# A float32 transformer encoder layer: where the last weight matrix is prepared, and how far ahead its raw pieces are loaded

## The chip, the cores and the metric

The kernel runs on one core of one Trainium2 chip. The metric is the time of one execution on the device in microseconds (us). The kernel before took 1673.07 us in the median of three runs (1670.78 to 1673.4).

## The reference, cut to what matters

One encoder layer runs on two sequences of 512 tokens, with a model width of 1024, all in float32. Three branches are computed from a common projection (a state space scan, a differential attention, and a cross attention to 256 memory tokens), gated, projected up and summed, and a gated feed-forward network with 2816 hidden units follows.

```python
def _layer(x, mem, l, p):
    xn = _rmsnorm(x, p['norm_mix'][l])
    mn = _rmsnorm(mem, p['norm_mem'][l])
    h = xn @ p['w_in'][l]
    u, q, k, v, xq, g = jnp.split(h, IN_SPLITS, axis=-1)
    y_s5 = _s5_branch(u, ...)                       # scan, gelu, GLU
    ...                                             # rope on q, k; differential attention
    mk, mv = jnp.split(mn @ p['w_mem_kv'][l], 2, axis=-1)
    y_x = _cross_attention(xq, mk, mv)
    merged = None
    for n in range(N_BRANCH):
        term = jax.nn.sigmoid(g[..., n * D_MODEL:(n + 1) * D_MODEL]) * (branches[n] @ p['w_up'][l, n])
        merged = term if merged is None else merged + term
    x = x + merged @ p['w_out'][l]
    xn2 = _rmsnorm(x, p['norm_ffn'][l])
    gate, up = jnp.split(xn2 @ p['w_ffn_in'][l], 2, axis=-1)
    return x + (jax.nn.silu(gate) * up) @ p['w_ffn_out'][l]
```

## The kernel before, in words

**Precision.** Matmuls take float32 operands as two parts, a rounded one and the rest (`wh`/`wl`, `xh`/`xl`), and a product is three matmuls: high by high, low by high, high by low. The helper `split` (L120 to L133) makes the two parts: the rounded one on ACT (L128, or L131 where a scale goes in), the rest on DVE (L129 or L132). All matmuls pass through one line, L61.

**Stages, in program order.** The scan branch; the gates (`gates`, products for the sigmoid gates that go to DRAM as `gD`); the GLU of the scan branch (four tiles, L460 to L469, `sg` to `bD`); the cross attention (35 steps, L618 to L655); the projections `q` and `k` of the differential attention, which are rotated (`rotated`, L672 to L686); the differential attention; the merge of the three branches; the output projection; the first feed-forward product (22 tiles `i`, L1050 to L1088); the second feed-forward product, which uses `w_ffn_out`.

**The prepared matrix.** The second feed-forward product multiplies 2 by 2 blocks with seven products instead of eight. For it `w_ffn_out` is needed as 36 pieces `(m, p)`, each of seven blocks: three of the four quadrants and four sums and differences of them, split in two parts each. The generator `prepare` (L399) makes one piece after another and stores it to DRAM (`wD`), from where the second product reads it hundreds of us later. One piece is:
- two loads into `raw` (L405, L406, 128 KB each, on SP's queue);
- a split of three quadrants into `hl` (128x3x128, thus 128x384 elements): ACT L131, then DVE L132; a store of 384 KB;
- four adds and subtracts on POOL, in place in `raw` (L415 to L418);
- a split of all four blocks of `raw` into a second `hl` (128x4x128, 128x512 elements): ACT L131, DVE L132; a store of 512 KB.

`raw` has one buffer, and so have the two `hl`. The generator stops (`yield`) once after the loads and once after the adds, so a piece is two half-pieces; each `half_piece()` call sets the next one into the program. The table `NPREP` says how many pieces are done by the end of the cross attention and how many by the end of the merge.

**Where half-pieces stand before.** Seven beside the seven last gate units, four beside the GLU tiles, 29 beside the 35 steps of the cross attention: 20 pieces. Eight in the merge of branch 2 (the loop `while queue`, L849 to L851), eight in the merge of branch 1 (L863 to L866): 8 pieces. Sixteen in the tiles 1 to 16 of the first feed-forward product: 8 pieces. Whatever is then left in the generator must be none.

**What sets the order.** Each engine runs its instructions in an order that a scheduler fixes when the program is built, from the written order, the pools and its costs. A tile that has no free buffer waits for the last reader of the buffer. After the cross attention PE goes on with the first rotated projection, into an accumulator bank (`bkmm`) that an earlier projection filled; that bank is free when its reader on DVE, the `stream_shuffle` of `rotated` (L681), has run:

```python
            V.tensor_tensor(out=t1, in0=o, in1=rope[0], op=ALU.mult)      # L679
            V.stream_shuffle(t2, o, mask)                                 # L681
            PO.tensor_tensor(out=t2, in0=t2, in1=rope[1], op=ALU.mult)    # L682
            PO.tensor_tensor(out=t1, in0=t1, in1=t2, op=ALU.add)          # L683
            split(hl[0][:, cs], hl[1][:, cs], t1, scale=0.125 if is_q else None)
```

**The merge.** A merge unit (`merge_units`, L707) is one of eight column tiles of one branch: 12 matmuls into each of two banks; DVE multiplies the gate `gl` by the two banks (L716, which frees the banks); POOL adds the result to `mg` (L720, 128x1024). The units of branch 2 have two banks for the products, those of branch 1 have six.

**The end of the first feed-forward product.** `quad_sums` (L899 to L902) makes the sums `ts` from the activations of the tiles 0 to 3 for the second product. Its pool `ts` opens where the pool `pq` of the preparation closes.

Of the kernel before, what the change touches and what calls it, by code (L numbers as in the profile page):

```python
# [10 lines left out]
F32 = mybir.dt.float32  # L11
# [8 lines left out]
P = 128  # L20
# [15 lines left out]
          (2, 6, 9), (3, 7, 9))  # L36
NPAIR = 9

NPREP = (20, 28)

NG = (7, 5, 7)
ROUND = 12582912.0
# [25 lines left out]
def encoder(ctx: ExitStack, tc: tile.TileContext, a, out):  # L68
# [88 lines left out]
    def proj(src, hi, lo, nk=KD, seqs=(0, 1)):  # L157


        wh, wl = weight(src, nk * P)  # L160
        outs = []
        for s in seqs:
            cs = slice(s * L, (s + 1) * L)
            outs.append(bank())
            for k in range(nk):
                mm3(outs[-1:], wh, wl, [(hi[k][:, cs], lo[k][:, cs])], k, nk)
        return outs
# [21 lines left out]
    def factor(ss, n, nt=4, bias=epsc):  # L189

        rs = rp.tile([P, 4], F32, tag="rs", name="rs", bufs=4)
        S.activation(out=rs[:, :nt], in_=ss[:, :nt], func=AF.Sqrt, scale=1.0 / n, bias=bias)
        V.reciprocal(rs[:, :nt], rs[:, :nt])
        bc = aux()
        for t in range(nt):
            PE.transpose(bc[:, t * P : (t + 1) * P], rs[:, t : t + 1].broadcast_to([P, P]), ident)
        return rs, bc
# [106 lines left out]
    _, bc = factor(ss0, DM)  # L304
# [12 lines left out]
    with yielding(last_s):  # L317
        x_norm(0, bc, range(6, 8))
        _, bc = factor(ss1, DM)
# [47 lines left out]
    def gates(n):  # L367

        for _ in range(n):
            t = next(todo)  # L370
            o = proj(a["w_in"][20 + t], xh, xl)
            gt = slot("ld", name="gt")
            for s in range(NS):
                cs = slice(s * L, (s + 1) * L)
                S.activation(out=gt[:, cs], in_=o[s], func=AF.Tanh, scale=0.5)
            nc.sync.dma_start(gD[t], gt)
# [19 lines left out]
    pieces = [(m, p) for m, lo_, hi_ in VISITS for p in range(lo_, hi_)]  # L396
    wD = {mp: drp.tile([P, 7, 2, P], F32, name=f"wD{mp[0]}_{mp[1]}") for mp in pieces}

    def prepare(es_, pieces_):  # L399
        pq = es_.enter_context(tc.tile_pool(name="pq", bufs=1, side="right", reuse_waits="tile"))  # L400
        for m, p in pieces_:
            raw = pq.tile([P, 4, P], F32, tag="raw", name="raw")
            f = slice(2 * p * P, (2 * p + 2) * P)
            with queued():
                nc.sync.dma_start(raw[:, 1:3], a["w_fo"][m, :, f].rearrange("p (a n) -> p a n", n=P))  # L405
                nc.sync.dma_start(raw[:, 0::3], a["w_fo"][m + 4, :, f].rearrange("p (a n) -> p a n", n=P))  # L406
            yield
            for j, w_ in ((4, raw[:, 1:4]), (0, raw)):
                n = w_.shape[1]
                hl = pq.tile([P, n, 2, P], F32R, tag=f"hl{n}", name="hl")  # L410
                split(hl[:, :, 0], hl[:, :, 1], w_, scale=0.5)
                nc.sync.dma_start(wD[m, p][:, j : j + n], hl.bitcast(F32))
                if j:
                    a21, a11, a12, a22 = (raw[:, i] for i in range(4))
                    PO.tensor_tensor(out=a22, in0=a21, in1=a22, op=ALU.add)  # L415
                    PO.tensor_tensor(out=a21, in0=a11, in1=a21, op=ALU.subtract)
                    PO.tensor_tensor(out=a11, in0=a22, in1=a11, op=ALU.subtract)
                    PO.tensor_tensor(out=a12, in0=a12, in1=a11, op=ALU.subtract)  # L418
                    yield

    def half_piece(behind_=()):
        with ExitStack() as es_:
            for i_ in behind_:
                es_.enter_context(tc.issue_after(i_.ins))
            return next(prep, None)
# [6 lines left out]
    for t in range(4):  # L432
# [9 lines left out]
        for s in range(NS):  # L442
            split(*(z_[t][:, s * L : (s + 1) * L].rearrange("p (j c) -> p j c", j=T) for z_ in (zh, zl)), yt[:, :, s, :], scale=0.5)
        zs.append(yt)
    pes = ExitStack()
    prep = prepare(pes, pieces[: NPREP[0]])
    next(prep)
    for _ in range(NG[2]):
        gates(1)
        half_piece()  # L450
    with behind():

        mrs = cst.tile([P, 4], F32, name="mrs")
# [6 lines left out]
    for t in range(4):  # L460
        o = proj(a["w_glu"][t], zh, zl, 4)
        sg = slot("zt", name="sg")
        for s in range(NS):
            S.activation(out=sg[:, s * L : (s + 1) * L], in_=o[s], func=AF.Tanh, scale=0.5, bias=bh[:, t : t + 1])
        for s in range(NS):
            g_ = sg[:, s * L : (s + 1) * L].rearrange("p (j c) -> p j c", j=T)
            V.scalar_tensor_tensor(out=g_, in0=g_, scalar=1.0, in1=zs[t][:, :, s, :], op0=ALU.add, op1=ALU.mult)
        nc.sync.dma_start(bD[0, t], sg)
        half_piece()  # L469
    phase.close()  # L470

    last_x = None
# [57 lines left out]
    xa = phase.enter_context(tc.tile_pool(name="xa", bufs=2, reuse_waits="tile"))  # L530
    xcol = phase.enter_context(tc.tile_pool(name="xcol", bufs=2, reuse_waits="tile"))

# [82 lines left out]
    for i in range(-AHEAD, len(steps) + 1):  # L618
# [24 lines left out]
        if i > 0 and steps[i - 1][2] == 3:  # L643
            h, s, _ = steps[i - 1]
# [201 lines left out]
    aes.close()  # L846
    prep = prepare(pes, pieces[NPREP[0] : NPREP[1]])
    next(prep)
# [14 lines left out]
    for m in range(KD):  # L863
        for _ in merge_units(1, b1, m, last=True):
            pass
        half_piece()  # L866
    assert next(prep, None) is None
    pes.close()

# [180 lines left out]
    for i in range(KFF):  # L1050
# [6 lines left out]
        if i == 1:  # L1057
            prep = prepare(pes, pieces[NPREP[1] :])
            next(prep)
# [11 lines left out]
        if i == 0:  # L1071
            for s in range(NS):
                _, bc = rstd(accs[s], DM)
# [539 lines left out]
```

## Time and profile before

| | |
|---|---|
| median of three runs | 1673.07 us |
| the profiled execution's own time | 1672.37 us |
| its span (first to last instruction) | 1670.6 us |
| mean granted TensorE clock | 0.984 |
| PE busy | 1595.8 us (96%) |
| DVE busy | 1180.5 us (71%) |
| ACT busy | 634.0 us (38%) |
| POOL busy | 554.0 us (33%) |
| DMA | 259.60 MB, mean 155 GB/s |

The span is cut into instructions of five engines: PE (matmuls, line L61), DVE, ACT, POOL and SP, which issues the DMAs. "Busy" counts only the time in which an engine executes. A row of a timeline has the start in us from the span's start, the duration in us, the engine, the line, the operation and the tiles (output <- inputs), the shapes, and in square brackets how long the engine sat idle before it and what ended that. A row of the waits has the engine and its instruction, what it waited for, the total in us, the number of times and the longest. A row of the windows has the window, its length, the busy time of PE, PEld (weight loads), DVE, ACT and POOL (instructions in brackets), the granted clock, the busy share of the DMA engines and GB/s.

### The profile page before, as it was taken

The numbers are of one execution on the slowest core, as the hardware profiler recorded it, in microseconds if no ns is written. First come the engines' busy times: TensorE is split into PE (matmuls) and PEld (weight loads), VectorE is DVE, ScalarE is ACT, GpSimd is POOL, SyncE is SP. The second block draws the span as 40 slices with busy tenths as digits, with TensorE's granted clock in tenths as the row PEclk, the third lists the DMA queues.
The fourth block names the chain that finished last, engine by engine and source line by source line (L and its number), as shares of the span: only waits on it lengthen the run. The fifth ranks groups of instructions, "written<-read, shape, count | busy, mean of one in ns | idle before, by whom it ended". The sixth has DMA issues, their size and how long they took to land.

```text
span 1670.6 us, 21694 instructions
## 1 busy us (share of the span) xinstructions
PE 1595.8 (96%) x7812; PEld 1315.4 (79%) x7812; DVE 1180.5 (71%) x1860; ACT 634.0 (38%) x1130; POOL 554.0 (33%) x444
## 2 busy tenths in 40 slices
PE   7999999998996699999999998999999999999997
PEld 5788788787895578877877886888888888788887
DVE  7956996255664377676568656988988888886455
ACT  6534313245453245565323434323332322321222
POOL 0001100031122322020066343665666665354242
PEclk9999999999998799999999999999999999999999
DMA  9354344768555211125577542343333322797632
GB/s 363 119 165 154 121 135 128 236 207 277 169 170 186 80 35 54 42 70 174 172 251 234 163 139 71 111 147 130 107 114 110 120 89 86 271 328 246 223 117 101
DMA packets 109354, 259.60 MB, mean 155 GB/s; under 512 B 14016, under 2 KB 42432, under 8 KB 109248
## 3 DMA queue, kind: packets, MB, share of 16 engines
q1 hardware_dynamic: 109248, 258.23, 46.0%
q8 instruction: 61, 1.00, 0.3%
q14 instruction: 45, 0.37, 0.1%
HBM read 174.85 MB, written 83.33 MB: 155 GB/s over the span
## 4 chain that ended last, share of the span: by engine, by line
PE 74%; DVE 10%; DMA 7%; ACT 3%; issue 2%; POOL 2%; SPq 1%; DVEq 0%; POOLq 0%; ACTq 0%
PE bkmm L61 63%; PE bktr L61 3%; DMA raw<-in_w_fo 3%; PE bksc L61 2%; PE bkoo L61 2%; PE bktr L64 2%; DVE wl L129 1%; DVE hl L132 1%; DMA yt<-bD 1%; PE bktr L1466 1%; ACT hl L131 1%; DVE st L1484 1%; ACT wh L128 1%; PE bktr L1437 1%; DVE tl L129 1%
## 5 line engine op out<-in xcount | busy, mean ns | idle before, releaser
L61 PE MATMUL bkmm<-xh,wh 128*128 128x512 f32 x640 | 256.8, 401 | 30.5 <-DVE t L681 27.2
L61 PE MATMUL bkmm<-xh,wl 128*128 128x512 f32 x640 | 251.8, 394 | 2.3 <-DVE wl L129 2.3
L61 PE MATMUL bkmm<-xl,wh 128*128 128x512 f32 x640 | 251.7, 393 | 0.0
L61 PE MATMUL bkmm<-tl,wh 128*128 128x512 f32 (+1 forms) x621 | 242.1, 390 | 3.5 <-DVE tl L129 3.5
L61 PE MATMUL bkmm<-th,wh 128*128 128x512 f32 (+1 forms) x621 | 242.2, 390 | 0.0
L61 PE MATMUL bkmm<-th,wl 128*128 128x512 f32 (+1 forms) x621 | 240.4, 389 | 0.6 <-DVE wl L129 0.6
L128 ACT CAST wh<-wf 128x1024 fp32r<-128x1024 f32 (+1 forms) x133 | 117.6, 884 | 196.6 <-PE bkmm L61 127.8
L129 DVE TENSOR_TENSOR wl<-wf,wh 128x1024 fp32r<-128x1024 f32 (+1 forms) x133 | 149.2, 1122 | 42.9 <-ACT wh L128 34.6
L61 PEld LDWEIGHTS bkmm<-xh,wh 128*128 128x128 f32 x640 | 120.9, 189 | 62.7 <-DVE t L681 27.9
L415 POOL TENSOR_TENSOR raw<-raw 128x128 f32<-128x128 f32 x36 | 24.2, 671 | 409.3 <-DVE hl L132 363.5
L61 PEld LDWEIGHTS bkmm<-xh,wl 128*128 128x128 f32 x640 | 120.9, 189 | 29.9 <-DVE wl L129 3.2
L61 PEld LDWEIGHTS bkmm<-tl,wh 128*128 128x128 f32 x621 | 117.1, 189 | 28.4 <-DVE tl L129 4.6
L61 PE MATMUL bkmm<-th,w 128*128 128x512 f32 x432 | 139.2, 390 | 0.1
L61 PEld LDWEIGHTS bkmm<-xl,wh 128*128 128x128 f32 x640 | 121.1, 189 | 22.5 <-issue 0.4
L61 PEld LDWEIGHTS bkmm<-th,wh 128*128 128x128 f32 x621 | 117.1, 189 | 25.0 <-ACT wh L128 1.2
L61 PEld LDWEIGHTS bkmm<-th,wl 128*128 128x128 f32 x621 | 116.7, 188 | 25.0 <-DVE wl L129 1.0
L132 DVE SCALAR_TENSOR_TENSOR hl<-raw,hl 128x384 fp32r<-128x384 f32 x72 | 76.6, 1064 | 77.3 <-ACT hl L131 76.8
L1081 POOL TENSOR_TENSOR up<-up,acc 128x512 f32<-128x512 f32 x44 | 84.6, 1942 | 93.7 <-DVE up L1027 93.7
L61 PEld LDWEIGHTS bkmm<-th,w 128*128 128x128 f32 x432 | 81.1, 188 | 17.7 <-DVE up L1027 0.8
L484 ACT ACTIVATE e<-bksc,nb 128x512 f32<-128x512 f32 (+1 forms) x96 | 58.6, 613 | 70.0 <-DVE nb L479 50.3
L61 PE MATMUL bkmm<-tl,w 128*128 128x512 f32 x216 | 84.1, 389 | 0.0
L131 ACT ACTIVATE hl<-raw 128x384 fp32r<-128x384 f32 x72 | 41.3, 573 | 103.6 <-DMA raw<-in_w_fo 68.4
(628 smaller groups left out, 3562.3 us busy)
## 6 DMA issues: line engine op xcount, KB each, us to landing
wf<-in_w_in SPq DMA_DIRECT2D x40, 512.0 KB, 3.9
wD<-hl SPq DMA_DIRECT2D x36, 512.0 KB, 2.9
w<-wD SPq DMA_DIRECT2D x36, 512.0 KB, 4.8
wD<-hl SPq DMA_DIRECT2D x36, 384.0 KB, 2.3
w<-wD SPq DMA_DIRECT2D x36, 384.0 KB, 3.4
gD<-gt SPq DMA_DIRECT2D x24, 512.0 KB, 2.9
gl<-gD SPq DMA_DIRECT2D x24, 512.0 KB, 4.3
wf<-in_w_fg SPq DMA_DIRECT2D x22, 512.0 KB, 3.5
```

Of the source, the lines that this page charges most:

```text
L61: return self.put(self.eng.matmul(*args, **kw))
L64: return self.put(self.eng.transpose(*args, **kw))
L128: h = S.copy(hi, src)
L129: l_ = V.tensor_tensor(out=lo, in0=src, in1=hi.bitcast(F32), op=ALU.subtract)
L131: h = S.activation(out=hi, in_=src, func=AF.Copy, scale=scale)
L132: l_ = V.scalar_tensor_tensor(out=lo, in0=src, scalar=scale, in1=hi.bitcast(F32), op0=ALU.mult, op1=ALU.subtract)
L415: PO.tensor_tensor(out=a22, in0=a21, in1=a22, op=ALU.add)
L484: last_x = S.activation(out=e, in_=sc, func=AF.Exp, bias=nb, scale=scale, accum_out=sm)
L1081: PO.tensor_tensor(out=up, in0=up, in1=accs[s], op=ALU.mult)
L1437: PE.matmul(kp[64 * hf : 64 * hf + 48, g * 144 : (g + 1) * 144], l_[:, 2 * hf + g, :], o_[:, 4 * g4 + 2 * hf + g, :], start=(l_ is lr48), ...
L1466: PE.matmul(ps[:, g * P : (g + 1) * P], w_[:, gg * P : (gg + 1) * P], u_[:, 8 * o + gg, :], start=True, stop=True)
L1484: V.tensor_tensor(out=sv[:, :, :, i], in0=p_, in1=q_, op=ALU.add)
```

## The change

`NPREP` goes from (20, 28) to (16, 27). The generator is opened just before the cross attention, and the gates and the GLU have no half-pieces beside them. `raw` gets two buffers, the first piece's loads are issued when the generator is opened, and the loads of piece n+1 are issued before the splits of piece n. The generator now also stops after the second half of a piece. So 32 half-pieces stand in the cross attention (16 pieces); the merge has 8 in its loop of branch 2 and up to 14 beside the units of branch 1 (11 pieces); the feed-forward tiles 1 to 18 have one each (9 pieces). What is loaded, computed and stored is the same in all.

```diff
-NPREP = (20, 28)
+NPREP = (16, 27)
...
     def prepare(es_, pieces_):
         pq = es_.enter_context(tc.tile_pool(name="pq", bufs=1, side="right", reuse_waits="tile"))
-        for m, p in pieces_:
-            raw = pq.tile([P, 4, P], F32, tag="raw", name="raw")
+        raws = []
+
+        def load(m, p):
+            raw = pq.tile([P, 4, P], F32, tag="raw", name="raw", bufs=2)
             f = slice(2 * p * P, (2 * p + 2) * P)
             with queued():
                 nc.sync.dma_start(raw[:, 1:3], a["w_fo"][m, :, f].rearrange("p (a n) -> p a n", n=P))
                 nc.sync.dma_start(raw[:, 0::3], a["w_fo"][m + 4, :, f].rearrange("p (a n) -> p a n", n=P))
-            yield
+            raws.append(raw)
+
+        load(*pieces_[0])
+        yield
+        for n_, (m, p) in enumerate(pieces_):
+            raw = raws[n_]
+            if n_ + 1 < len(pieces_):
+                load(*pieces_[n_ + 1])
             for j, w_ in ((4, raw[:, 1:4]), (0, raw)):
                 n = w_.shape[1]
...
                     PO.tensor_tensor(out=a12, in0=a12, in1=a11, op=ALU.subtract)
-                    yield
+                yield
...
-    pes = ExitStack()
-    prep = prepare(pes, pieces[: NPREP[0]])
-    next(prep)
-    for _ in range(NG[2]):
-        gates(1)
-        half_piece()
+    gates(NG[2])
...
         nc.sync.dma_start(bD[0, t], sg)
-        half_piece()
     phase.close()
...
+    pes = ExitStack()
+    prep = prepare(pes, pieces[: NPREP[0]])
+    next(prep)
...
         for _ in merge_units(1, b1, m, last=True):
             pass
         half_piece()
+        if m < 6:
+            half_piece()
     assert next(prep, None) is None
     pes.close()
```

The scheduler's orders of the two programs are nearly the same on PE. On the other engines they differ above all at three places. (Numbers behind a tile's name count the tiles of one program and are no line numbers; lines after L530 stand some lines further down in the changed program.)

**ACT at the end of the cross attention**, before: `hl` are splits of pieces, `xpTh` the transposed probabilities of the cross attention, `xosb` its last output copy, `rh` the first rotated projection.

```order
L131 ACTIVATE hl_4733<-raw_4685 128x3x128
L128 CAST wh_5339<-wf_5337 128x1024
L128 CAST xpTh_5138<-bktr_5209 128x2x128
L131 ACTIVATE hl_4795<-raw_4685 128x4x128
L653 COPY xosb_5221<-bkoo_5214 128x512
L131 ACTIVATE hl_4834<-raw_4799 128x3x128
L131 ACTIVATE hl_4887<-raw_4799 128x4x128
L131 ACTIVATE hl_4938<-raw_4891 128x3x128
L131 ACTIVATE hl_4989<-raw_4891 128x4x128
L131 ACTIVATE hl_5038<-raw_4993 128x3x128
L131 ACTIVATE hl_5091<-raw_4993 128x4x128
L131 ACTIVATE rh_5244<-t1_5246 128x512
```

ACT in the changed program, at the same place:

```order
L131 ACTIVATE hl_5089<-raw_5008 128x3x128
L659 COPY xosb_5086<-bkoo_5079 128x512
L487 ACTIVATE e_5104,sm_5105<-bksc_5097,nb_5101 128x256
L128 CAST xpTh_5066<-bktr_5117 128x2x128
L131 ACTIVATE hl_5128<-raw_5008 128x4x128
L128 CAST xpTh_5066<-bktr_5138 128x2x128
L128 CAST wh_5279<-wf_5277 128x1024
L128 CAST xpTh_5066<-bktr_5149 128x2x128
L659 COPY xosb_5161<-bkoo_5154 128x512
L131 ACTIVATE rh_5184<-t1_5186 128x512
```

Before, six splits (three pieces) stand between the last copy of the cross attention and the first rotated part, and DVE has the six second halves of them in the same place. In the changed program none stands there, on ACT or on DVE, and DVE has the first pair L679/L681 of `rotated` ahead of its last `xpTl` (the rest of the transposed probabilities).

**DVE in the merge units of branch 2**, before: `gl` frees a bank, `hl` is a piece's split, `wl` the rest of a weight tile.

```order
L716 SCALAR_TENSOR_TENSOR gl_7936<-gl_7936,bkmm_7944 128x512
L132 SCALAR_TENSOR_TENSOR hl_8017<-raw_7933,hl_8017 128x4x128
L716 SCALAR_TENSOR_TENSOR gl_7936<-gl_7936,bkmm_7958 128x512
L129 TENSOR_TENSOR wl_8030<-wf_8027,wh_8029 128x512
L716 SCALAR_TENSOR_TENSOR gl_7981<-gl_7981,bkmm_7989 128x512
L132 SCALAR_TENSOR_TENSOR hl_8061<-raw_8021,hl_8061 128x3x128
L716 SCALAR_TENSOR_TENSOR gl_7981<-gl_7981,bkmm_8003 128x512
L129 TENSOR_TENSOR wl_8075<-wf_8072,wh_8074 128x512
```

and in the changed program:

```order
L722 SCALAR_TENSOR_TENSOR gl_7876<-gl_7876,bkmm_7884 128x512
L132 SCALAR_TENSOR_TENSOR hl_7960<-raw_7873,hl_7960 128x4x128
L132 SCALAR_TENSOR_TENSOR hl_8004<-raw_7912,hl_8004 128x3x128
L722 SCALAR_TENSOR_TENSOR gl_7876<-gl_7876,bkmm_7898 128x512
L129 TENSOR_TENSOR wl_7970<-wf_7967,wh_7969 128x512
L722 SCALAR_TENSOR_TENSOR gl_7924<-gl_7924,bkmm_7932 128x512
L132 SCALAR_TENSOR_TENSOR hl_8093<-raw_8001,hl_8093 128x3x128
L132 SCALAR_TENSOR_TENSOR hl_8049<-raw_7912,hl_8049 128x4x128
L722 SCALAR_TENSOR_TENSOR gl_7924<-gl_7924,bkmm_7946 128x512
L129 TENSOR_TENSOR wl_8018<-wf_8015,wh_8017 128x512
```

One split stood in a unit before; where these rows are, two stand in a unit now. Ahead of the first `gl` of branch 1 DVE has 17 splits in the changed program and 11 before: all three pieces that the merge gains come into the units of branch 2, although their calls are written beside branch 1.

**DVE at the end of the first feed-forward product**, before: `ac`, `u2` and `gf` belong to a tile's result, `ts` are the sums of `quad_sums`.

```order
L132 SCALAR_TENSOR_TENSOR hl_12028<-raw_11727,hl_12028 128x4x128
L1083 TENSOR_TENSOR ac_12016<-ac_12016,up_11984 128x512
L1027 TENSOR_TENSOR u2_12086<-bkmm_12073,p1_12071 128x512
L899 TENSOR_TENSOR ts_12649<-fa_12645 128x512
L899 TENSOR_TENSOR ts_12658<-fa_12654 128x512
L901 TENSOR_TENSOR ts_12649<-fb_12646,ts_12649 128x512
```

and in the changed program, two tiles later:

```order
L132 SCALAR_TENSOR_TENSOR hl_12318<-raw_11860,hl_12318 128x4x128
L1091 TENSOR_TENSOR ac_12306<-ac_12306,up_12274 128x512
L1035 TENSOR_TENSOR u2_12383<-bkmm_12370,p1_12368 128x512
L907 TENSOR_TENSOR ts_12649<-fa_12645 128x512
L907 TENSOR_TENSOR ts_12658<-fa_12654 128x512
L909 TENSOR_TENSOR ts_12649<-fb_12646,ts_12649 128x512
```

Both `quad_sums` follow the last split of the last piece in either program; they stand in tile 17 before and in tile 19 now.

## The prediction

> **What bounds the kernel now.** I began with the page: busy times, the chain that ended last, the costliest groups.
>
> ```profile
> PE 1595.8 (96%) x7812; PEld 1315.4 (79%) x7812; DVE 1180.5 (71%) x1860; ACT 634.0 (38%) x1130; POOL 554.0 (33%) x444
> PE bkmm L61 63%; PE bktr L61 3%; DMA raw<-in_w_fo 3%; PE bksc L61 2%; PE bkoo L61 2%; PE bktr L64 2%; DVE wl L129 1%; DVE hl L132 1%; DMA yt<-bD 1%; PE bktr L1466 1%; ACT hl L131 1%; DVE st L1484 1%; ACT wh L128 1%; PE bktr L1437 1%; DVE tl L129 1%
> L131 ACT ACTIVATE hl<-raw 128x384 fp32r<-128x384 f32 x72 | 41.3, 573 | 103.6 <-DMA raw<-in_w_fo 68.4
> ```
>
> PE sets the end, with 96% busy. What is odd is a load in the chain: `raw<-in_w_fo` has 3% of it, and ACT sat 68.4 us before its piece splits until that load had landed. So I asked what PE waited for.
>
> ```profile
> PE bkmm L61 <- DVE t L681: 27.2, 1, 27.2
> PE bktr L61 <- ACT wh L128: 8.0, 1, 8.0
> PE bkmm L61 <- DVE wl L129: 5.9, 10, 1.2
> PE bkmm L61 <- ACT wh L128: 2.3, 2, 1.2
> PE bkmm L61 <- ACT sg L464: 2.1, 1, 2.1
> PE bkmm L61 <- DVE gl L716: 1.8, 2, 1.4
> ```
>
> One wait of 27.2 us, met once, is by far the largest. The timelines of PE, DVE and ACT around it:
>
> ```profile
> 555.55 0.79 PE L61 MATMUL bkmm<-xh,wh 128*128 128x512 f32 x1 [27.21 <-DVE t L681]
> 561.68 0.40 PE L61 MATMUL bkmm<-xh,wl 128*128 128x512 f32 x1
> 561.91 0.40 PE L61 MATMUL bkmm<-xh,wh 128*128 128x512 f32 x1
> ```
> ```profile
> 553.55 0.69 DVE L132 SCALAR_TENSOR_TENSOR hl<-raw,hl 128x512 fp32r<-128x512 f32 x1 [2.88 <-ACT hl L131]
> 554.16 0.68 DVE L679 TENSOR_TENSOR t<-bkmm,rc 128x512 f32<-128x512 f32 x1
> 554.77 0.72 DVE L681 STREAM_SHUFFLE t<-bkmm 128x512 f32<-128x512 f32 x1
> 560.23 0.73 DVE L681 STREAM_SHUFFLE t<-bkmm 128x512 f32<-128x512 f32 x1
> ```
> ```profile
> 541.16 0.52 ACT L131 ACTIVATE hl<-raw 128x384 fp32r<-128x384 f32 x1 [4.42 <-DMA raw<-in_w_fo]
> 544.49 0.63 ACT L131 ACTIVATE hl<-raw 128x512 fp32r<-128x512 f32 x1 [2.80 <-POOL raw L418]
> 549.57 0.52 ACT L131 ACTIVATE hl<-raw 128x384 fp32r<-128x384 f32 x1 [4.44 <-DMA raw<-in_w_fo]
> ```
>
> The shuffle that frees PE's bank stands on DVE behind the last piece's second split. At the end of the cross attention three pieces are still to be split, and nothing else is left to do. They come every 549.57 - 541.16 = 8.4 us: 3.3 us from the first split to the second (541.16 to 544.49, POOL's adds between them), 0.6 us of the second, and then 4.4 us in which ACT waits for the next load, which can't be issued while the one `raw` buffer is still being read. So the wait is a chain of pieces, and half of each piece is the load.
>
> **The change part by part.** The sum is made against the profiled execution's 1672.37 us, which is 0.7 below the median of the runs (1673.07).
>
> *The wait.* No piece's split is left between the cross attention and the rotated projection in the new orders. The bank's reader is a pair of DVE instructions (0.68 and 0.72 us) whose input was finished long before, so the whole wait goes: -27.2. Were three pieces still late, each would take the 4.0 us without its load, 12 us in all.
>
> *The slow clock behind it.* After the wait PE needs 561.68 - 555.55 = 6.13 us for 14 matmuls; at the later spacing of 561.91 - 561.68 = 0.23 us they take 3.2. The granted clock of that window is 0.78:
>
> ```profile
> 450.00:500.00 50.00, 50.00 (x323) 44.81 (x322) 35.04 (x103) 27.10 (x73) 9.86 (x21) 1.00 0.54 182
> 500.00:550.00 50.00, 26.35 (x153) 22.09 (x152) 19.71 (x49) 17.18 (x39) 11.02 (x20) 0.78 0.53 181
> 412.00:528.00 116.00, 113.45 (x660) 97.75 (x659) 78.43 (x224) 56.92 (x147) 23.18 (x44) 1.00 0.50 167
> 828.00:876.00 48.00, 45.48 (x197) 36.46 (x196) 31.25 (x36) 12.91 (x20) 30.23 (x27) 1.00 0.80 254
> ```
>
> Without the wait PE stays at 1.00, as at 450 to 500: -2.9.
>
> *The bank at the switch.* L679 and L681 now stand ahead of the last `xpTl`, for which PE waits: at most their 0.68 + 0.72 = 1.4 us if they come at the worst moment, nothing if DVE is ahead. The second shuffle comes 560.23 - 554.77 = 5.5 us after the first, and PE's 24 matmuls on the first bank take 24 x 0.23 = 5.5, so the two keep pace. I take +1, from 0 to 1.4; a second bank that is late by a whole round (5.5) is a rival.
>
> *The denser cross attention.* From 412 to 528 PE is busy 113.45 of 116 us. ACT has 59 us idle there, DVE 37.
>
> ```profile
> L131 ACT ACTIVATE hl<-raw 128x512 fp32r<-128x512 f32 x12 | 7.5, 629 | 8.8 <-POOL raw L418 8.8
> L132 DVE SCALAR_TENSOR_TENSOR hl<-raw,hl 128x512 fp32r<-128x512 f32 x11 | 7.6, 691 | 2.5 <-ACT hl L131 2.4
> ```
>
> These groups of that window show 11 to 12 pieces in it; 16 come now. Four and a half more cost ACT 4.5 x (0.63 + 0.52) = 5.2 us and DVE 4.5 x (0.69 + 0.56) = 5.6 us, within the idle time. A piece may take (528 - 419) / 16 = 6.8 us (the first split can come some 7 us after the stage starts); it takes 8.4 - 4.4 = 4.0 without the load. The loads are two DMAs more per piece ahead in SP's queue; the DMA share is 0.50. I take 0. With the cover gone it would cost up to 4.5 x 1.25 = 5.6.
>
> *The gates and the GLU.* Eleven half-pieces go from there. One of them holds up ACT:
>
> ```profile
> 378.52 0.53 ACT L131 ACTIVATE hl<-raw 128x384 fp32r<-128x384 f32 x1 [4.53 <-DMA raw<-in_w_fo]
> 405.29 0.50 PE L61 MATMUL bkmm<-xh,wh 128*128 128x512 f32 x1 [2.11 <-ACT sg L464]
> ```
>
> ACT's `wh` behind that split is late for PE by 1.1 us (one of the two waits of 2.3 us above). The 2.1 us for `sg` come from a store of the GLU behind the pieces' stores, which may be quicker without them. I take -2, from 0 to -4.
>
> *The merge.* Three pieces more come into the units of branch 2, where only two banks are open, so a late `gl` stops PE soon. DVE is busy 31.25 of 48 us and POOL 30.23, so by busy time there is room; but they get into each other's way:
>
> ```profile
> 847.76 0.56 DVE L132 SCALAR_TENSOR_TENSOR hl<-raw,hl 128x384 fp32r<-128x384 f32 x1 [2.44 <-ACT hl L131]
> 851.24 2.89 DVE L132 SCALAR_TENSOR_TENSOR hl<-raw,hl 128x512 fp32r<-128x512 f32 x1
> 850.80 2.78 POOL L720 TENSOR_TENSOR mg<-mg,gl 128x1024 f32<-128x1024 f32 x1 [0.26 <-DMA wD<-hl]
> 867.75 0.47 PE L61 MATMUL bkmm<-yh,wh 128*128 128x512 f32 x1 [1.44 <-DVE gl L716]
> L129 DVE TENSOR_TENSOR wl<-wf,wh 128x512 fp32r<-128x512 f32 x8 | 5.5, 685 | 0.0
> L129 DVE TENSOR_TENSOR yl<-yt,yh 128x1024 fp32r<-128x1024 f32 x3 | 3.7, 1225 | 2.7 <-ACT yh L128 2.7
> L418 POOL TENSOR_TENSOR raw<-raw x36: 453/462/1495, 337.6 to 1336.9; 128x128 f32<-128x128 f32 x36
> ```
>
> A split alone takes 0.56 us; one that meets POOL's `mg` add takes 2.89 and ends with it. So I count DVE's instructions with two inputs in SBUF and POOL's as one queue. In 828 to 876 that is POOL's 30.23, `wl` 5.5, `yl` 3.7 and eight splits at their free 0.56 and 0.69 (5.0): 44.4 of 48 us. Three pieces add 3 x (0.56 + 0.69 + four adds of 0.46) = 9.3. Of these 3.6 fit, 5.7 do not: +6. Below it, 0 (all hidden in the 16.75 us that DVE is idle); above, 9.3 if nothing fits. I stay at 6, since the queue is nearly full. The DMAs come near their limit too: 254 GB/s over 48 us are 12.2 MB at a share of 0.80, and three pieces add 3 x (0.25 + 0.38 + 0.51) = 3.4 MB, so 1.03 of 48 us, or 0.91 of 54. That is no more than the +6 and lies beside it, so I don't add it.
>
> The Trainium skill, "SBUF — State Buffer", section "Who interferes with whom", says that a VectorE instruction with two SBUF inputs and a GpSimd instruction that reads SBUF share a port pair, locked for the whole instruction, the later one blocked. By that rule the sum is the +6 of one queue, by busy time alone it would be 0; the 2.89 beside 0.56 agrees with the rule.
>
> *The end of the first product.* `ts` moves from tile 17 to 19, closer to the last tile.
>
> ```profile
> 1362.53 0.68 DVE L1027 TENSOR_TENSOR p<-bkmm,u 128x512 f32<-128x512 f32 x1
> 1379.52 0.67 DVE L1027 TENSOR_TENSOR p<-bkmm,u 128x512 f32<-128x512 f32 x1
> 1396.58 0.68 DVE L1027 TENSOR_TENSOR p<-bkmm,u 128x512 f32<-128x512 f32 x1
> 1414.77 0.69 DVE L1027 TENSOR_TENSOR p<-bkmm,u 128x512 f32<-128x512 f32 x1 [1.05 <-PE bkmm L61]
> ```
>
> A tile takes PE 84 x 0.227 = 19.0 us. Counted back from the last row, where DVE waits for PE, DVE is 4.9, 2.8 and 0.85 us late in the three rows before. Shifted by two tiles, it is 2.8 late in tile 20, and tile 21, which takes seven banks at once, needs DVE caught up. I take +2, from 0 (the free banks absorb it) to 2.8. The ninth piece beside the tiles I count as nothing: it adds 1.2 us to DVE's 17 in each of two tiles of 19.0.
>
> Sum: -27.2 - 2.9 + 1 + 0 - 2 + 6 + 2 = -23.1, so 1649.3 in a profiled execution, and 1650 in the median. With every term at its good end (-27.2 - 2.9 - 4) it is 1639; at its bad end (+1.4, +5.6, 0, +9.3, +2.8, hence -11) 1662.
>
> **The rivals.**
>
> *The merge queue serialises (10%).* If each of the six extra splits meets an `mg` add as that at 851.24 did, each takes 2.89 - 0.69 = 2.2 us more, 13.2, and its piece's adds (3 x 1.84 = 5.5) come on top: +18.7 instead of 6, about 1663. For it: where one split stood beside a bank's `gl`, two do now. Against it: `gl`, with one input in PSUM, runs beside POOL, and PE lost only 1.8 us to it before.
>
> *The rotated projection's second bank (5%).* The stall goes, but DVE's order at the switch, with `rl` between two shuffles, makes the second bank late by a round: +5.5, 1655 to 1656. Against it: the two paces are equal.
>
> *The chain keeps its pace (5%), the other side.* What if the load is not what paces a piece, but the single `hl` buffers, whose stores must land before the next split, or the loads still come late in SP's queue? Then a piece stays at 8.4 us; 16 end at 419 + 134 = 553, and the wait is about 25 us instead of 27.2. The clock loss stays, and the rest adds up to -2.2 - 2 + 6 + 2 = +4: 1677, slower. This decides from 6.8 us per piece on. Against it: the wait named in every piece is the load, 4.4 us, and the page's stores land in 2.9 and 2.3 us, within a piece of 4.
>
> ```profile
> wD<-hl SPq DMA_DIRECT2D x36, 512.0 KB, 2.9
> wD<-hl SPq DMA_DIRECT2D x36, 384.0 KB, 2.3
> ```
>
> **How the numbers follow.** My forecast has 80%, at 1650, with its own range of 1640 to 1660. The range is 1640 to 1662: it takes in the second-bank case and part of the merge case. About 0.2% (3.3 us) is what a measurement of this kernel can tell from no change. Forecast, merge and second-bank cases are all faster; in the last case it is slower, or just the same if the merge and the last tiles cost nothing. So faster 0.94, same 0.02, slower 0.04.
>
> **What would show it.** PE's wait for `DVE t L681` (its new line number is some lines further down) must be gone or below 1.5 us, the clock in 500 to 550 back at 1.00, and ACT's wait for `raw` far below 68.4 us. The piece period in the cross attention must be below 6.8 us. In the merge of branch 2 splits of over 2 us become more, and PE's loss <- `gl` L716 grows by about 6. In tile 20 or 21 a new wait of about 2 us for a DVE `L1035` result appears. A `raw` wait still near 4.4 us per piece would prove the forecast wrong.

## The result

The changed kernel took 1649.89 us in the median of four runs (1648.71 to 1651.51), the kernel before 1672.46 us beside it (1670.78 to 1673.4). The ratio is 0.9867, with a 95% interval of 0.985 to 0.9884: 22.6 us faster. The prediction was 1650 us, faster with a chance of 0.94. The profiled execution took 1648.71 us, its span is 1646.9 us.

To see where the time went I cut each span at the starts of certain matmuls on PE, whose order is nearly the same in all kernels: the first of the GLU (`zh`), the first scores of the cross attention (`bksc`), its last output product (`bkoo<-xpTh,mkvl`), the first and the last product of the merge (`yh`/`yl`), the first and the last product of the two feed-forward matrices with `th`. The table has the us between them, from one profiled execution of each kernel; the names of the lower rows are those of the experiments below.

| | GLU | cross attention | switch, rotation, attention | merge | then | feed-forward |
|---|---|---|---|---|---|---|
| before | 37.7 | 111.4 | 237.1 | 155.9 | 88.5 | 638.3 |
| changed | 33.1 | 111.2 | 206.5 | 162.8 | 87.3 | 643.4 |
| difference | -4.6 | -0.2 | -30.6 | +6.9 | -1.2 | +5.1 |
| e1_one_raw | 33.1 | 116.7 | 225.1 | 160.1 | 88.3 | 644.1 |
| e2_ahead_only | 33.1 | 110.5 | 208.0 | 158.8 | 88.5 | 639.0 |
| e3_cross19 | 33.1 | 111.3 | 212.1 | 157.8 | 88.4 | 643.4 |
| e4_ffn_front | 33.1 | 112.0 | 208.4 | 162.9 | 87.3 | 640.3 |
| e5_cross22 | 33.8 | 110.5 | 207.9 | 157.6 | 87.3 | 639.7 |
| e6_no_adds | 33.1 | 112.0 | 208.5 | 161.2 | 88.4 | 642.3 |
| e7_after_again | 33.1 | 112.0 | 207.2 | 162.1 | 87.3 | 643.9 |
| e8_ahead_again | 34.0 | 109.9 | 206.5 | 159.2 | 88.4 | 638.7 |
| e9_no_stores | 33.1 | 112.0 | 208.3 | 166.9 | 87.3 | 643.9 |
| e10_hl2 | 33.1 | 112.0 | 207.1 | 160.5 | 87.3 | 642.5 |
| e11_ahead_hl2 | 33.1 | 110.2 | 206.5 | 155.5 | 87.9 | 638.6 |
| e12_merge_empty | 33.1 | 112.0 | 208.5 | 149.6 | 87.3 | 644.4 |

What lies ahead of the GLU and behind the last column differs by less than 1 us between before and changed. Two profiles of one program (changed and e7, e2 and e8) differ by up to 1.5 us in a column, so that a single difference of 1 us says nothing.

### The profile page after: what moved, and what is told of

It is laid out like the page before. It is cut to its first block, busy times and chain, and to the rows that moved or that the text cites. A ratio compares the mean times of both kernels' runs of the same rounds, so it can differ in the third digit from the quotient of the medians.

```text
span 1646.9 us, 21707 instructions
## 1 busy us (share of the span) xinstructions
PE 1597.5 (97%) x7812; PEld 1317.8 (80%) x7812; DVE 1175.2 (71%) x1860; ACT 633.5 (38%) x1130; POOL 550.4 (33%) x444
## 4 chain that ended last, share of the span: by engine, by line
PE 79%; DVE 10%; DMA 3%; issue 2%; POOL 2%; ACT 2%; SPq 1%; DVEq 0%; POOLq 0%; ACTq 0%
PE bkmm L61 68%; PE bktr L61 3%; PE bksc L61 2%; PE bkoo L61 2%; PE bktr L64 2%; DVE wl L129 2%; DVE st L1492 1%; PE bktr L1474 1%; POOL mg L726 1%; POOL up L1089 1%; DMA yt<-bD 1%; DVE hl L132 1%; DVE xt L243 0%; DMA wD<-hl 0%; DMA raw<-in_w_fo 0%
## 5 line engine op out<-in xcount | busy, mean ns | idle before, releaser
L132 DVE SCALAR_TENSOR_TENSOR hl<-raw,hl 128x384 fp32r<-128x384 f32 (+1 forms) x72 | 72.9, 1016 | 24.0 <-ACT hl L131 23.9
L61 PE MATMUL bkmm<-yh,wh 128*128 128x512 f32 x192 | 78.0, 407 | 3.3 <-DVE gl L722 2.9
```

The source lines that it names most:

```text
L61: return self.put(self.eng.matmul(*args, **kw))
L132: l_ = V.scalar_tensor_tensor(out=lo, in0=src, scalar=scale, in1=hi.bitcast(F32), op0=ALU.mult, op1=ALU.subtract)
```

## The profile after

The page's line of engines, and PE's largest waits (engine and line, what was waited for, total us, times, longest):

```profile
PE 1597.5 (97%) x7812; PEld 1317.8 (80%) x7812; DVE 1175.2 (71%) x1860; ACT 633.5 (38%) x1130; POOL 550.4 (33%) x444
```
```profile
PE bkmm L61 <- DVE wl L129: 10.3, 9, 3.4
PE bktr L61 <- ACT wh L128: 8.1, 1, 8.1
...
PE bkmm L61 <- DVE gl L722: 2.9, 2, 2.5
...
PE bkoo L61 <- DVE xpTl L129: 2.0, 1, 2.0
```

The 27.2 us for the shuffle are not in the list any more. `wl` has grown from 5.9 to 10.3 us, `gl` from 1.8 to 2.9, and `xpTl` from 0.9 to 2.0. ACT's group of splits, in the view by lines, and two windows of the changed kernel (the columns as explained above), and two rows of ACT's timeline:

```profile
L131 ACT ACTIVATE hl<-raw 128x384 fp32r<-128x384 f32 (+1 forms) x72 | 40.7, 572 | 49.8 <-POOL raw L427 24.7 <-DMA wD<-hl 23.9 <-DMA raw<-in_w_fo 1.2
```
```profile
500.00:550.00 50.00, 47.01 (x231) 38.56 (x229) 26.53 (x57) 18.74 (x38) 14.82 (x18) 1.00 0.39 135
412.00:530.00 118.00, 115.01 (x670) 99.98 (x669) 80.63 (x222) 62.80 (x159) 36.54 (x68) 1.00 0.62 214
```

```profile
413.73 0.51 ACT L131 ACTIVATE hl<-raw 128x384 fp32r<-128x384 f32 x1
...
512.12 0.53 ACT L131 ACTIVATE hl<-raw 128x384 fp32r<-128x384 f32 x1 [1.43 <-DMA wD<-hl]
```

ACT's wait for a raw load fell from 68.4 us to 1.2 us. What a split waits for now is POOL's adds, or the store of the piece before out of the single `hl` buffer (`wD<-hl`, 23.9 us). The granted clock in 500 to 550 is 1.00, before it was 0.78. The last two rows are the first splits of the first and of the sixteenth piece in the cross attention, so a piece comes every (512.12 - 413.73) / 15 = 6.6 us.

Two places lost time. The first is the start of the last unit of branch 2 in the merge, just ahead of the border to branch 1; the timelines of PE, DVE and POOL there:

```profile
834.01 0.77 PE L61 MATMUL bkmm<-yh,wh 128*128 128x512 f32 x1 [2.55 <-DVE gl L722]
834.58 0.63 PE L61 MATMUL bkmm<-yl,wh 128*128 128x512 f32 x1
835.00 0.63 PE L61 MATMUL bkmm<-yh,wl 128*128 128x512 f32 x1
...
837.72 0.40 PE L61 MATMUL bkmm<-yh,wh 128*128 128x512 f32 x1
837.95 0.39 PE L61 MATMUL bkmm<-yl,wh 128*128 128x512 f32 x1
```
```profile
831.09 2.18 DVE L132 SCALAR_TENSOR_TENSOR hl<-raw,hl 128x512 fp32r<-128x512 f32 x1 [2.09 <-ACT hl L131]
833.19 0.67 DVE L722 SCALAR_TENSOR_TENSOR gl<-gl,bkmm 128x512 f32<-128x512 f32 x1
```
```profile
830.35 2.37 POOL L726 TENSOR_TENSOR mg<-mg,gl 128x1024 f32<-128x1024 f32 x1
```

The read `gl`, which frees PE's bank, stands on DVE behind a split. The split first waited 2.09 us for ACT and then ran for 2.18 us instead of 0.69, until POOL's `mg` add had ended. In branch 1 a wait of 2.31 us follows, for a weight's rest `wl` that took 2.84 us beside the next `mg` add; such rows of 128x512 take 0.68 us elsewhere:

```profile
875.44 0.79 PE L61 MATMUL bkmm<-yh,wl 128*128 128x512 f32 x1 [2.31 <-DVE wl L129]
```
```profile
872.55 2.84 DVE L129 TENSOR_TENSOR wl<-wf,wh 128x512 fp32r<-128x512 f32 x1
```
```profile
871.51 3.33 POOL L726 TENSOR_TENSOR mg<-mg,gl 128x1024 f32<-128x1024 f32 x1 [1.23 <-DVE gl L722]
```

Waits are only about half of what the merge lost. The window of the merge in the kernel before, and in the changed kernel:

```profile
764.80:920.70 155.90, 150.54 (x707) 120.72 (x707) 107.06 (x144) 61.45 (x120) 57.00 (x46) 1.00 0.65 208
729.40:892.20 162.80, 154.32 (x707) 122.23 (x706) 108.91 (x153) 63.48 (x125) 64.85 (x59) 0.98 0.67 225
```

PE idles 162.80 - 154.32 = 8.5 us instead of 155.90 - 150.54 = 5.4, thus 3.1 us more. For the same 707 matmuls it is busy 3.8 us longer, most of it because after each of the two waits they come at half speed for some 3 us; the granted clock of the window fell from 1.00 to 0.98.

The second place is the last tile of the first feed-forward product, again on PE:

```profile
1397.13 0.79 PE L61 MATMUL bkmm<-th,wl 128*128 128x512 f32 x1 [3.45 <-DVE wl L129]
```

## The experiments

**One raw buffer.** The changed kernel with one number undone:

```diff
-            raw = pq.tile([P, 4, P], F32, tag="raw", name="raw", bufs=2)
+            raw = pq.tile([P, 4, P], F32, tag="raw", name="raw", bufs=1)
```

> The changed kernel with one edit: raw has one buffer again (places and counts of the pieces stay 16, 11 and 9). Theory (the load behind the one buffer paces the pieces): a piece takes about 8.4 us again, 16 pieces end near 550 us, PE waits 22 to 27 us for the shuffle of the rotated projection and loses about 3 us more at a low clock: about 1675 us, 1668 to 1681. Rival (the smaller number and the new places of the pieces are what removed the wait): the wait stays below 5 us, 1650 to 1655 us.

It took 1671.36 us, a ratio to the kernel before of 0.9985 (0.9976 to 0.9994), so nearly the whole gain is gone. PE's wait, two of ACT's rows and the window:

```profile
PE bkmm L61 <- DVE t L687: 16.3, 1, 16.3
```
```profile
533.39 0.52 ACT L131 ACTIVATE hl<-raw 128x384 fp32r<-128x384 f32 x1 [2.00 <-DMA raw<-in_w_fo]
541.07 0.52 ACT L131 ACTIVATE hl<-raw 128x384 fp32r<-128x384 f32 x1 [3.73 <-DMA raw<-in_w_fo]
```
```profile
500.00:550.00 50.00, 29.95 (x151) 24.00 (x150) 22.43 (x54) 18.56 (x42) 15.26 (x26) 0.77 0.53 192
```

The splits wait for their loads again, a piece takes 541.07 - 533.39 = 7.7 us, and the low clock (0.77) is back. The wait is 16.3 us and not 22 to 27, since two pieces are left at the end and not three; the cross attention itself lost 5.5 us more. So the new number and places of the pieces alone turn a wait of 27.2 us into one of 16.3 and 5.5 us lost ahead of it; the second buffer removes both. The rival falls.

**The loads ahead alone.** The kernel before, with the generator of the changed kernel and nothing else: `NPREP` stays (20, 28), the half-pieces stay beside the gates and the GLU.

```diff
     def prepare(es_, pieces_):
         pq = ...
-        for m, p in pieces_:
-            raw = pq.tile([P, 4, P], F32, tag="raw", name="raw")
...
+        load(*pieces_[0])
+        yield
+        for n_, (m, p) in enumerate(pieces_):
+            raw = raws[n_]
+            if n_ + 1 < len(pieces_):
+                load(*pieces_[n_ + 1])
```

> The kernel before with one edit: two buffers of raw and the next piece's loads ahead of the splits; all places and counts as before (11 half-pieces beside gates and GLU, 20, 8 and 8 pieces). Theory: the wait of 27 us and the slow clock behind it go (-30.6, +1 at the switch), and the merge (6.9 us less loss than in the changed kernel) and the last tiles (about 4 less) stay as before: about 1643 us, 1638 to 1649, thus faster than the whole change. Rival (the places do it): the splits beside the gates go on holding up ACT and pieces are left at the end of the cross attention: 1655 us or more.

It took 1642.32 us, ratio 0.9807 (0.9786 to 0.9828): faster than the whole change. Its repetition beside the changed kernel:

> The changed kernel unedited, beside the others on one chip, so that differences of 2 to 3 us can be read: 1648 to 1652 us.

> The kernel before with the loads one piece ahead and nothing else, unedited from its first run, beside the changed kernel on one chip: 1640 to 1644 us, 6 to 9 us below the changed kernel if the first comparison holds. Of these 4 come from the merge and 4 to 5 from the last feed-forward tiles.

These gave 1651.22 us (1649.43 to 1652.6) for the changed kernel and 1641.55 us (1639.95 to 1643.35) for the loads ahead alone, thus 9.7 us between them. In the table the two pairs differ by 2.9 to 4.0 us in the merge and by 4.4 to 5.2 in the feed-forward column. So moving pieces out of the gates and into the merge and the feed-forward tiles cost time, and all of the gain comes from the load ahead. The GLU tells the same: it takes 33.1 us with half-pieces beside it and loads ahead (34.0 in the repetition), and 33.1 us without them and one buffer (e1). Either edit alone gives the 4.6 us, or 3.7 of them in the repetition.

**Three pieces from the merge to the cross attention.**

```diff
-NPREP = (16, 27)
+NPREP = (19, 27)
...
         half_piece(last_e)
+        if i < 1:
+            half_piece(last_e)
...
         half_piece()
-        if m < 6:
-            half_piece()
```

> The changed kernel with three of the merge's 11 pieces moved to the cross attention: 19, 8 and 9 pieces, 38 half-pieces in its 35 steps. Theory (three pieces more in two-bank merge units cost some 7 us there): the loss of PE in the merge falls by 5 to 7 us, and the cross attention takes 19 pieces at 5.7 us each without a stall: about 1643 us; up to 1648 if the last piece comes late at the switch. Rival (the merge's loss has another source, such as its place in time): the merge keeps its loss, 1650 us.

It took 1654.44 us (ratio 0.9883, 0.9864 to 0.9902), above the range expected. The merge fell to 157.8 us, by the 5 us that the theory says, but what it gave back was lost at the switch:

```profile
528.52 0.79 PE L61 MATMUL bkmm<-xh,wh 128*128 128x512 f32 x1 [3.84 <-DVE t L689]
```
```profile
523.14 0.55 DVE L132 SCALAR_TENSOR_TENSOR hl<-raw,hl 128x384 fp32r<-128x384 f32 x1
526.53 0.69 DVE L132 SCALAR_TENSOR_TENSOR hl<-raw,hl 128x512 fp32r<-128x512 f32 x1 [2.84 <-ACT hl L131]
527.14 0.68 DVE L687 TENSOR_TENSOR t<-bkmm,rc 128x512 f32<-128x512 f32 x1
```

The second split of one piece is late, and the shuffle (now L689) stands behind it. It is the old wait with one piece instead of three.

**The feed-forward pieces two tiles earlier.**

```diff
             half_piece((last_t, last_sum))
+            if i < 3:
+                half_piece((last_t, last_sum))
```

> The changed kernel with one edit: two half-pieces instead of one in the first two tiles of the first feed-forward product, so that the nine pieces end two tiles earlier and the sums ts stand in tile 17 as in the kernel before. Theory (ts two tiles later is what PE's new wait of 3.45 us in the last tiles comes from): the wait goes, 1645.5 to 1647 us. Rival (the ninth piece itself is too much for DVE): the loss stays or moves to other tiles, 1649 to 1652 us.

It took 1647.87 us (ratio 0.9837, 0.9816 to 0.9859). The whole time is 2.0 and 3.4 us below the two series of the changed kernel, a little less than expected. The trace is clearer: the wait of 3.45 us is gone (0.62 us is left), and the feed-forward column falls by 3.1 us. I compared the time between two fixed `th` products, some 340 and 470 us after the first: the changed kernel takes 4.3 us more there than the kernel before, this one 0.4 us less. Some 95 us after the first product 1 us is lost that the changed kernel did not lose. So the end of the preparation, two tiles too late, is the cause of that wait. The edit moves the last splits and the sums `ts` together and does not tell them apart. What the ninth piece itself costs is within the 1.3 to 1.6 us by which this column still exceeds the two of the loads ahead alone (639.0 and 638.7).

**POOL's adds left out in the merge.** The sums of 11 pieces are not computed:

```diff
-                if j:
+                if j and adds:
```

> The changed kernel without POOL's four adds for the 11 pieces of the merge (the sums of these pieces are left out, so the second splits take the raw blocks); all splits, loads and stores stay. Theory (DVE's splits and POOL's work exclude each other, one queue of 44 + 9 us in 48): with 11 x 1.84 = 20 us of POOL's work gone the merge of the three branches, 162.8 us from its first to its last product in the changed kernel, falls by 5 to 9 us, and fewer splits of over 2 us are left. Rival (DVE's own time, two splits between the two reads of the banks): the merge stays at 161 to 163 us.

It took 1649.06 us. The merge is 161.2 us, 0.9 to 1.6 less than in the changed kernel; as many splits of over 2 us are left (five). POOL's busy time in the merge falls from 65 to 37 us, and PE's idle time there does not fall: it is 10.3 us, beside 8.5 and 7.9 in the two profiles of the changed kernel. So the sum of DVE's and POOL's work is not what the merge's length follows. My theory of one queue falls here, as a sum. The `mg` adds stay in this kernel, so what a single split or `wl` loses beside one of them is not tested by it.

**The stores left out in the merge.** The other candidate was the DMA traffic.

```diff
-                nc.sync.dma_start(wD[m, p][:, j : j + n], hl.bitcast(F32))
+                if store:
+                    nc.sync.dma_start(wD[m, p][:, j : j + n], hl.bitcast(F32))
+                else:
+                    wD[m, p] = wD[pieces[0]]
```

> The changed kernel without the stores of the merge's 11 pieces (22 stores, 9.9 MB; the second product reads the first piece in their place, so these pieces' result is left out). Loads, splits and adds stay. Theory now (the merge loses because the pieces' chain of stores and loads is late on nearly full DMA queues, and gl and yl stand behind the splits on DVE): the merge of the branches falls from 162.8 or 162.1 us to 154 to 158. Rival 1 (the port queue of DVE and POOL): POOL and DVE have the same work, so it stays at 161 to 163. The FFN tiles keep their 643 us in both.

It took 1653.6 us, and the merge got longer, 166.9 us; neither my range nor that of the rival has that. A window of branch 2 shows that the traffic is gone (the share of the DMA engines is 0.42; in the changed kernel it is 0.83 from 792 to 840), and still PE loses:

```profile
796.00:844.00 48.00, 42.22 (x173) 33.66 (x171) 27.30 (x35) 11.88 (x21) 29.16 (x31) 0.93 0.42 132
```

One of its waits, followed back through PE, DVE, ACT and SP's queue:

```profile
828.78 0.50 PE L61 MATMUL bkmm<-yh,wh 128*128 128x512 f32 x1 [3.03 <-DVE gl L725]
```
```profile
827.57 0.56 DVE L132 SCALAR_TENSOR_TENSOR hl<-raw,hl 128x384 fp32r<-128x384 f32 x1 [5.04 <-ACT hl L131]
828.04 0.68 DVE L725 SCALAR_TENSOR_TENSOR gl<-gl,bkmm 128x512 f32<-128x512 f32 x1
```
```profile
827.01 0.52 ACT L131 ACTIVATE hl<-raw 128x384 fp32r<-128x384 f32 x1 [8.02 <-DMA raw<-in_w_fo]
```
```profile
821.95 0.33 SPq L140 DMA_DIRECT2D wf<-in_w_up  x1
822.33 0.42 SPq L407 DMA_DIRECT2D raw<-in_w_fo  x1
```

DVE had nothing to do for 5.04 us, and the finished product of PE lay in its bank. But `gl` stands behind a split whose load SP had issued only at 822.33, behind a weight load (`wf`). In the list of SP's waits from 790 to 843 these weight loads waited 24.1 us in all for a free weight buffer:

```profile
SPq L140 <- DVE wl L129: 24.1, 7, 5.5
```

So DVE waits for the input of an instruction that nobody needs soon, and what PE needs stands behind it. "Loads ahead" in the written order were not ahead on SP's queue there. This is the chain of this kernel, whose order without stores is another one. In the changed kernel the weight loads waited 2.4 us from 785 to 845, and ACT's splits waited 1.2 us for a load from 785 to 885, but 21.3 us for the stores out of `hl` and 20.3 us for POOL's adds. So taking the traffic away does not shorten the merge, and which input is late depends on the kernel.

**Two `hl` buffers in the merge**, in the changed kernel and in the one with the loads ahead alone:

```diff
-                hl = pq.tile([P, n, 2, P], F32R, tag=f"hl{n}", name="hl")
+                hl = pq.tile([P, n, 2, P], F32R, tag=f"hl{n}", name="hl", bufs=nh)
...
-    prep = prepare(pes, pieces[NPREP[0] : NPREP[1]])
+    prep = prepare(pes, pieces[NPREP[0] : NPREP[1]], 2)
```

> The changed kernel with two buffers each for the two hl tiles in the merge's pieces alone: a split no longer waits for the store of the piece before; the traffic stays. If it is the wait for the single hl buffers (8.9 us of ACT in branch 2), the merge falls by 2 to 5 us, 1645 to 1648 us in all. If it is the traffic or the port pair, it stays within 1 us of 162.5 and 1650 us in all.

> The kernel before with the loads one piece ahead, and two buffers of hl in the merge's 8 pieces: if the single hl buffers make the wait of 3.6 us at the end of branch 2, the merge falls from 159 us to 155 or 156, and the time to 1637 to 1640 us; else 1641 to 1643.

The first took 1649.16 us (0.9856, 0.9839 to 0.9873), its merge 160.5 us, 1.6 to 2.3 less than without: at the edge of what the trace can tell. Its window shows that PE idles no less, 160.60 - 151.18 = 9.4 us instead of 8.5; what is gone is the low clock:

```profile
732.00:892.60 160.60, 151.18 (x707) 120.22 (x706) 113.74 (x153) 63.84 (x126) 66.61 (x59) 1.00 0.68 229
```

From 785 to 885 ACT's splits wait 5.5 us instead of 21.3 for the stores out of `hl`, but 16.2 instead of 1.2 for the loads. The second took 1640.66 us (0.9797, 0.9778 to 0.9817), its merge 155.5 us, 3.3 to 3.7 less than without, and PE's longest wait for `gl` is 1.6 us; with one `hl` buffer (e2) it was 3.6, at the last unit of branch 2:

```profile
PE bkmm L61 <- DVE gl L725: 2.0, 2, 1.6
```

With it went a low clock that had followed the wait (granted 1.00 in the merge instead of 0.98); PE's idle time fell by 0.9 to 1.4 us only, to 5.2 from 6.1 and 6.6. So with eight pieces the second `hl` buffers took away the one long wait and the slow matmuls behind it; with eleven they did not lessen PE's waits. It is the fastest kernel here that does the whole computation, but its time lies within 2 us of the loads ahead alone, which their spread doesn't separate.

**Two more pieces in the cross attention.** The kernel with the loads ahead alone, but 22, 6 and 8 pieces:

```diff
-NPREP = (20, 28)
+NPREP = (22, 28)
...
-        half_piece()
+        if m < 4:
+            half_piece()
```

> The kernel before with the loads one piece ahead, and two of the merge's eight pieces moved into the cross attention: 22 pieces by its end (11 half-pieces beside gates and GLU, 33 beside the cross attention), 6 in the merge, 8 beside the feed-forward tiles. Theory (each piece taken out of the merge gives back 1.3 to 1.6 us there, and a piece in the cross attention costs nothing as long as it takes under 6.8 us): the merge falls by about 3 us against the version with the loads ahead alone, 1637 to 1641 us. Rival (the cross attention is full, or a piece is late at its end): 1642 us or more, with a wait of PE for the shuffle of the rotated projection.

It took 1641.24 us (0.981, 0.9796 to 0.9825), beside 1641.55 of e8 on the same chip: no difference in the whole, just above the theory's range, and without the rival's wait for the shuffle. The merge is 1.2 to 1.6 us shorter, which the other stages take back in its one trace.

**No piece in the merge.** The 11 pieces are left out, and the second product reads the first piece in their place:

```diff
-    prep = prepare(pes, pieces[NPREP[0] : NPREP[1]])
-    next(prep)
+    for mp in pieces[NPREP[0] : NPREP[1]]:
+        wD[mp] = wD[pieces[0]]
+    prep = iter(())
```

> The changed kernel with no piece in the merge at all (its 11 pieces are left out; the second product reads the first piece in their place). The floor of the merge. Theory now (what PE loses in the merge are reads of its banks and rests of weights that stand on DVE, in its fixed order, behind splits whose input is late): no wait of PE of over 1.5 us for gl or wl is left, and the merge of the branches takes 151 to 154 us against 162.5, so that 11 pieces cost 9 to 11 us there, near 1 us each; 1639 to 1643 us in all. Rival (the loss at the border of the two branches, where the banks are laid out anew, is there without pieces too): the wait of 2.5 us at that border stays, 156 us or more.

It took 1637.54 us. The merge's floor is 149.6 us, below my range as is the whole time, and in its window PE waits only for this:

```profile
PE bktr L64 <- DVE e L783: 0.9, 1, 0.9
PE bkmm L61 <- DVE gl L722: 0.2, 1, 0.2
```

The border and the unit ahead of it are free of a wait, so the rival falls. The pieces cost the merge 155.9 - 149.6 = 6.3 us before (eight of them), 13.2 us in the changed kernel (eleven), 9.2 to 9.6 with eight and the loads ahead, and 5.9 when `hl` has two buffers as well.

## Why the prediction was right, point by point

**The bound, the wait and the clock** (-27.2 and -2.9) were right in mechanism and size: the stage from the switch to the merge fell by 30.6 us against 30.1 forecast. That the load behind the one buffer paces the pieces is shown by e1, that the load ahead suffices alone by e2. The new number and places of the pieces, without it, left 16.3 of the 27.2 us and lost 5.5 in the cross attention. The rival that the chain keeps its pace is out.

**The switch** (+1): `xpTl` is waited for 2.0 us instead of 0.9, so +1.1, and the second bank was not late.

**The cross attention** (0): 111.2 us against 111.4, with 16 pieces every 6.6 us. But "one piece may take 6.8 us, it takes 4.0" was too hopeful as a measure of room. In e3, with 19 pieces (5.7 us each), one was late at the switch; its last half-piece is written beside the last step. The pieces follow the steps of the stage, they don't run at their own 4.0 us.

**The gates and the GLU** (-2, from 0 to -4): -4.6. The step that failed is "eleven half-pieces go from there" as the cause: the load ahead gives the same with the half-pieces in place. I had taken the 2.11 us for `sg` as a matter of the stores in part; all of it went in e2 with the same stores, and all but 0.6 us in e8. Why that store of the GLU landed sooner there I have not taken apart.

**The merge** (+6, from 0 to 9.3): +6.9, but the step behind it, one queue of DVE's and POOL's instructions that is filled to 44.4 of 48 us and takes 9.3 more, was not the mechanism. Taking 20 us out of it in e6 changed 0.9 to 1.6 us and did not lessen PE's idle time. Nor did the signs come that I had named: splits of over 2 us became fewer (five instead of seven in the merge, four instead of five ahead of the first `gl` of branch 1), and PE's loss for `gl` grew by 1.1 us and not by 6. What the rows show is DVE's fixed order: a bank's read or a weight's rest stands behind a split that is late, be it for POOL's adds, the `hl` buffer's store or a load. The blocked pair of DVE and POOL is there in single rows and lengthens the two longest waits: 2.18 us instead of 0.69 ahead of that `gl`, 2.84 instead of 0.68 for that `wl`. (The prediction set 2.89 us beside the 0.56 of a smaller split; a split of the same shape takes 0.69.) How the waits divide between the late input and the blocked pair no run separates. And of the 6.9 us only 3.1 are waiting: the rest is mainly PE's clock behind the two long waits (some 1.5 us each), a term that I had put at nothing in the merge, without a reason. The rival of a merge that serialises (+18.7) used the same sum and falls with it.

Even the load ahead itself costs here: with eight pieces the merge went from 155.9 to 158.8 and 159.2 us, which no step of mine had. In e2 15 of the 16 splits stand ahead of the first `gl` of branch 1, in the kernel before 11; with eleven pieces and one buffer (e1) it is 12 of 22. So the crowd in the units of branch 2, 17 splits in the changed kernel, comes mostly with the load ahead and not with the three pieces more. PE idles only 0.8 to 1.3 us more in these two; most of the loss is the clock after one wait of 3.6 us.

**The last tiles** (+2, from 0 to 2.8): between the two `th` products named with e4, +4.3. The mechanism, the sums `ts` and the last splits two tiles later, is shown by e4. The term was too small: the wait is 3.45 us, for `wl` and not for a result of L1035 as I had written, and the matmuls behind it run at half speed for some 3 us, which costs 1.6 and which I had priced only at the switch.

The forecasts of the GLU (2.6 us too high) and of the last tiles (2.3 us too low) cancel, and the merge's size is right for another reason. The total of 1650 us owes something to that.

## What to carry to other kernels

When an engine that works ahead has its wait on a load in a chain of pieces, take the load ahead first and measure that alone, before moving work about: here the load ahead with its second buffer alone gave 31 us, and moving the pieces with it gave 9.7 of these back. Work that is off the critical path is not free on an engine with a fixed order, however idle the engine is: ask what stands behind each such instruction, and when its input comes. Ahead in the written order is not ahead on the queue of the transfers.

## What I had not expected of the hardware

PE slowed down after waits far shorter than that of 27 us. After the 2.55 us in the merge matmuls come every 0.43 us (834.58 to 835.00) until 837.5 and then every 0.23; that costs some 1.6 us on top of the wait, and the same follows the 2.31 us at 875.44 and the 3.45 us in the last tile. In the kernel before, PE's wait of 1.44 us at the same unit (867.75) was followed by this:

```profile
868.06 0.39 PE L61 MATMUL bkmm<-yl,wh 128*128 128x512 f32 x1
868.29 0.40 PE L61 MATMUL bkmm<-yh,wl 128*128 128x512 f32 x1
```

These come every 0.23 us at once. The length of the wait alone does not decide: with two `hl` buffers (e10) a wait of 2.56 us left the clock as it was, and again the matmuls come every 0.23 us:

```profile
882.67 0.50 PE L61 MATMUL bkmm<-yh,wl 128*128 128x512 f32 x1 [2.56 <-DVE wl L129]
883.01 0.39 PE L61 MATMUL bkmm<-yh,wh 128*128 128x512 f32 x1
883.24 0.39 PE L61 MATMUL bkmm<-yl,wh 128*128 128x512 f32 x1
```

The Trainium skill, "TensorE: Matmul & The Clock Gate", section "What's actually happening", gives an idle window of about 3.4 us, free-running, after which the clock is halved; the 2.31 and 2.55 us here are shorter than that window, and the measurement decides: a wait of 2.3 us can cost the clock too, and one of 2.56 us need not. What sets the difference no run here shows.
